# A preamble in another order on VectorE and ScalarE, and the keys' norm table of both layers in one chain

## The chip, the core and the metric

One core of one Trainium2 chip runs the whole program. The metric is the device time of one execution in microseconds; the time of a kernel is the median of its runs. Engines are named as the profile names them: PE is TensorE, DVE is VectorE, ACT is ScalarE, POOL is GpSimd, SP is SyncE, which here only issues DMAs.

## The reference

A trunk of two layers on 512 tokens of width 2048, in float32. Each layer norms its input, makes one input projection, feeds three branches and adds one output projection to the residual stream:

```python
def _layer(x, norm_g, w_in, conv_w, conv_b, sb_qn_g, sb_kn_g, gla_w_up, gla_b_up, gla_on_g, w_out):
    h = _rmsnorm(x, norm_g)
    proj = h @ w_in
    (cv_h, cv_b, cv_c, cv_g, sb_q, sb_k, sb_v, sb_g,
     gl_q, gl_k, gl_v, gl_g, gl_lr) = jnp.split(proj, split_points, axis=-1)
    y_conv = _short_conv(cv_h, cv_b, cv_c, conv_w, conv_b) * silu(cv_g)
    q = _rmsnorm(sb_q.reshape(b, s, SB_HEADS, SB_HD), sb_qn_g)
    k = _rmsnorm(sb_k.reshape(b, s, SB_HEADS, SB_HD), sb_kn_g)
    y_sb = _stick_breaking(q, k, v) * silu(sb_g)
    g = log_sigmoid(gl_lr @ gla_w_up + gla_b_up) / GLA_TAU
    y_gla = _rmsnorm(_gla(gl_q, gl_k, gl_v, g), gla_on_g) * silu(gl_g)
    return x + concatenate([y_conv, y_sb, y_gla]) @ w_out

def _rmsnorm(x, g):
    return x * lax.rsqrt(jnp.mean(x * x, axis=-1, keepdims=True) + EPS) * g
```

The stick-breaking branch has 8 heads of 128; the gated linear attention (GLA) has 4 heads, and its value columns and low-rank columns are the first that the kernel computes.

## The kernel before

**Numbers.** Every float32 factor of a large product is kept as two f16 parts, a high one (`xh`, `wh`) and the residual below it (`xl`, `wl`). A product is three f16 products: high by high, low by high, high by low. Before it is split, a group of weights is scaled by a power of two that comes from its own sum of squares.

**Weight groups.** The weights come in groups of 256 columns in the order of `specs`: per layer 30 groups of `w_in` and 8 of `w_out`. Group 0 is the first half of GLA's values, group 1 the second half with the 16 low-rank columns (tile `kT`), group 2 GLA's queries. A group lands in one of two staging buffers `st` as two halves of 8 blocks of 128 rows (`fetch`, the first three on SP's queue, the others on POOL's). Then, for each group: squares and their sums on ACT (`wmax`, L383; L388 for the narrow columns), a sum over partitions on POOL (L399), four tiny steps to the scale on DVE (`wscale`, L401 to L417), and per half the high part on ACT (`whi`, L454, L456) and the residual on DVE (`wlo`, L461, L464). Group 0 has steps of its own: `wpeak0` (L430 and L433) for its bound, products on PE in place of POOL (L409), and `whi0` (L445 on ACT, L447 on DVE), quarter by quarter.

**Tokens.** The 512 tokens are four tiles of 128. For tile t the preamble makes: the sum of squares (`xsquare`, L630, ACT), the norm's factor (`xnorm`, two steps on ACT and five tiny ones on DVE), the gain, per half of the width (`xgain`, L581, DVE), the transposition of a half by 8 matmuls against the identity into one of two PSUM buffers `psz` (`xhigh`, L591, PE), the copy of that half to f16 `xh` (L593, ACT), and the residual `xl` (`xlow`): for tile 0 PE subtracts the copy in PSUM (L603) and ACT copies (L604), for the other tiles DVE subtracts (L600). A PSUM buffer is free once the residual is made.

**Order.** On DVE and ACT the preamble's steps stand in the order in which the code calls them, from `byhand` (L107) to its end (L684). Everything else, PE included, and DVE's and ACT's later steps among those of the preamble, is placed by a planner, once, when the program is built; an engine then runs its list in order and waits at each step for what the step needs. `order(a, b)` makes the planner put a behind b on one engine, without a wait of its own. The planner deals PE the matmuls of `project_by_token` (L857; groups 0 and 1, all four tiles) between the transposes. Group 2 and what follows is weights by columns (`project_cols`, L702 to L704).

**Around it.** `layer_consts` (L292) turns the small parameters (L294, L295) and makes, for each layer, the table `kg` that the queries of the attention are multiplied by (L1414, near 324 us): a product of two gain vectors, its maximum over partitions on POOL (L183), a power of two below it, a reciprocal, a diagonal, and one product on PE against ones (L310), copied by L311. It is called behind group 0. `xsums` makes sums of token quarters for later products (L735 on DVE, L743 on ACT, 12 and 4 steps in each half of `steps`). `split_v` (L948, L949) takes GLA's values out of PSUM. `weights` (L537) fetches the group two further on.

## Time and profile before

| | us |
|---|---|
| median of 3 runs | 1634.72 |
| lowest and highest | 1633.69, 1635.13 |
| the profiled execution | 1635.55 |
| its span | 1633.8 |

The span runs from the first to the last instruction that the profiler saw; 1.75 us lie around it. A row of a timeline gives the start in the span, the length, the engine, the line, the operation with tiles written and read, the shape, how many instructions are merged in it, and in brackets the engine's idle time before it with what ended that. The length of a matmul counts until its result is out, so the pitch of matmuls is read from start to start. A row of merged instructions can have waits inside it only if they are short.

### The profile page before, as it was taken

To read this page: it belongs to the slowest core of one execution; us is meant where nothing else is said; L and a number is where in the kernel's file an instruction comes from. 1 tells how busy PE (TensorE), PEld (TensorE's weight loads), DVE (VectorE), ACT (ScalarE), POOL (GpSimd) and SP (SyncE) were. 2 spreads that over 40 slices of the span, in tenths; PEclk is the share of its full clock that TensorE was granted. 3 is DMA by queue.
4 is the path that set the end of the run, shared out by engine and by line. 5 is a ranking of instruction groups with operands and counts; after the bars stand their busy time and mean duration, and the time that the engine had idled before them with its cause. 6 is when DMAs were issued, how large, how long until landed. Compare 5 with 4: busy or idle time off the path is not lost.

```text
span 1633.8 us, 42252 instructions
## 1 busy us (share of the span) xinstructions
PE 1615.5 (99%) x18202; PEld 1356.8 (83%) x18202; DVE 1446.2 (89%) x2417; ACT 1196.5 (73%) x1771; POOL 269.4 (16%) x306
## 2 busy tenths in 40 slices
PE   8999999999999999999999999999999999999998
PEld 5757768989899968799996668689898989668998
DVE  7989989989898979898699899898998889898896
ACT  7668887977777776756775697788786868676573
POOL 0122021111212122011102111212121211220110
PEclk9999999999999999999999999999999999999999
DMA  7244435477767686644743544545777786773441
GB/s 262 81 103 145 89 119 111 106 164 144 169 150 169 150 169 186 177 148 147 244 94 107 127 117 103 144 89 137 155 158 160 153 165 150 161 229 130 156 157 54
DMA packets 193643, 235.98 MB, mean 144 GB/s; under 512 B 90242, under 2 KB 153036, under 8 KB 192944
## 3 DMA queue, kind: packets, MB, share of 16 engines
q0 software_dynamic: 79904, 181.42, 42.2%
q1 hardware_dynamic: 104544, 42.42, 13.4%
q10 hardware_dynamic: 9008, 9.45, 1.8%
q8 instruction: 142, 2.33, 0.6%
q14 instruction: 45, 0.37, 0.1%
HBM read 179.65 MB, written 14.68 MB: 119 GB/s over the span
## 4 chain that ended last, share of the span: by engine, by line
PE 68%; DVE 16%; ACT 7%; DMA 5%; issue 3%; POOL 1%; SPq 0%; DVEq 0%; ACTq 0%; POOLq 0%
PE psp L798 22%; PE psp L795 13%; PE psp L857 6%; PE psp L714 4%; PE psp L713 4%; PE psp L715 4%; PE psp L703 3%; PE psp L702 3%; DVE wl L509 3%; PE psp L704 3%; DMA st<-in_w_in_dram 3%; ACT wh L508 1%; PE psm L1345 1%; ACT junk L383 1%; PE psz L1305 1%
## 5 line engine op out<-in xcount | busy, mean ns | idle before, releaser
L508 ACT ACTIVATE wh<-st,ws 128x1024 f16<-128x1024 f32 x270 | 300.7, 1144 | 170.5 <-DVE st L528 89.8
L509 DVE SCALAR_TENSOR_TENSOR wl<-st,ws,wh 128x1024 f16<-128x1024 f32 x270 | 340.3, 1283 | 28.4 <-ACT wh L508 28.3
L383 ACT ACTIVATE junk<-st 128x2048 uint8<-128x2048 f32 x150 | 285.4, 1903 | 14.7 <-DMA st<-in_w_out_dram 6.9
L795 PE MATMUL psp<-s,wh 128*128 128x256 f16 x1280 | 217.7, 273 | 1.0 <-DVE g L811 0.9
L795 PEld LDWEIGHTS <-wh 128*128 128x128 f16 x1920 | 187.4, 98 | 23.3 <-issue 1.4
L798 PE MATMUL psp<-wh,s 128*128 128x128 f16 x2048 | 177.1, 219 | 0.5 <-issue 0.4
L795 PE MATMUL psp<-s,wl 128*128 128x256 f16 x640 | 174.3, 273 | 0.9 <-DVE wl L509 0.9
L713 PE MATMUL psp<-wh,m 128*128 128x256 f16 x640 | 174.5, 273 | 0.0
L715 PE MATMUL psp<-wh,m 128*128 128x256 f16 x640 | 174.5, 273 | 0.0
L714 PE MATMUL psp<-wl,m 128*128 128x256 f16 x640 | 174.5, 273 | 0.0
L798 PEld LDWEIGHTS <-s 128*128 128x128 f16 x3072 | 173.0, 98 | 0.8 <-issue 0.7
L798 PE MATMUL psp<-wl,s 128*128 128x128 f16 x1024 | 173.3, 219 | 0.0
L461 DVE SCALAR_TENSOR_TENSOR wl<-st,ws,wh 128x2048 f16<-128x2048 f32 x62 | 145.0, 2349 | 15.0 <-ACT wh L454 13.8
L362 POOL DMA_DIRECT2D st<-in_w_in_dram x114 | 109.7, 1030 | 246.4 <-DVE w7l L509 118.3
L798 PEld LDWEIGHTS <-m 128*128 128x128 f16 x2448 | 139.1, 98 | 2.1 <-issue 1.6
L454 ACT ACTIVATE wh<-st,ws 128x2048 f16<-128x2048 f32 x60 | 118.6, 1999 | 16.0 <-DVE ws L415 7.9
L399 POOL PARTITION_ALL_REDUCE wgm<-wm x75 | 48.1, 641 | 461.2 <-ACT junk L383 446.0
L386 POOL DMA_DIRECT2D st<-st x36 | 57.2, 1590 | 350.8 <-ACT junk L383 331.5
L795 PEld LDWEIGHTS <-wl 128*128 128x128 f16 x960 | 93.9, 98 | 14.4 <-issue 2.1
L798 PE MATMUL psp<-wh,m 128*128 128x128 f16 x1088 | 97.2, 219 | 0.4 <-DVE ws L415 0.4
L798 PE MATMUL psp<-wl,m 128*128 128x128 f16 x544 | 93.0, 219 | 0.0
L704 PEld LDWEIGHTS <-wl 128*128 128x128 f16 x384 | 37.6, 98 | 44.6
(448 smaller groups left out, 4193.5 us busy)
## 6 DMA issues: line engine op xcount, KB each, us to landing
st<-in_w_in_dram POOLq DMA_DIRECT2D x114, 1024.0 KB, 8.4
st<-in_w_out_dram POOLq DMA_DIRECT2D x32, 1024.0 KB, 8.3
st<-st POOLq DMA_DIRECT2D x36, 512.0 KB, 6.6
st<-in_w_in_dram SPq DMA_DIRECT2D x6, 1024.0 KB, 12.0
mixd<-g POOLq DMA_DIRECT2D x20, 256.0 KB, 7.6
x<-in_x_dram SPq DMA_DIRECT2D x4, 1024.0 KB, 5.2
qT<-in_x_dram ACTq DMA_DIRECT2D x8, 512.0 KB, 4.1
qT<-xs ACTq DMA_DIRECT2D x8, 512.0 KB, 12.2
```

What stands on the lines that cost most here:

```text
L362: load = queue.dma_start(s_, src[l, h * HK * P:(h + 1) * HK * P, c0:c0 + GW].rearrange("(k p) n -> p k n", p=P), max_dma_last_dim=1024)
L383: sq = S.activation(junk(HK * GW).rearrange("p (k n) -> p k n", k=part.shape[1]), part, AF.Square, accum_out=peak[i][:, h:h + 1])
L454: hi = S.activation(wh[:, :, :GW], staged[i][h], AF.Copy, scale=scales[i])
L461: a = V.scalar_tensor_tensor(wl[:, :, :GW], staged[i][h], scales[i], wh[:, :, :GW], ALU.mult, ALU.subtract)
L508: hi = S.activation(h_, b, AF.Copy, scale=sc)
L509: V.scalar_tensor_tensor(l_, b, sc, h_, ALU.mult, ALU.subtract)
L713: T.matmul(o, ah[:, t, k, :], wh[:, kk, :n], start=st_, stop=False, skip_group_check=True)
L714: T.matmul(o, ah[:, t, k, :], wl[:, kk, :n], start=False, stop=False, skip_group_check=True)
L715: return T.matmul(o, al[:, t, k, :], wh[:, kk, :n], start=False, stop=en, skip_group_check=True)
L795: mm = T.matmul(o, w[q_][:, kk, :], a[p_][:, :, kk, :], start=st_, stop=en, skip_group_check=True)
L798: mm = T.matmul(o[:, t * P:(t + 1) * P], a[p_][:, t, kk, :], w[q_][:, kk, :], start=st_, stop=en, skip_group_check=True)
L857: mm = T.matmul(o[:, :n], a_[:, t, k, :], w[k // HK][part][:, k % HK, :n], start=i == 0 and k == 0, stop=i == 2 and k == KT - 1)
```

## The change

Four edits, all in the first layer's preamble and first two groups.

- *Start.* The second half of token tile 0 is copied to f16 by DVE (L602) and not by ACT, ahead of group 0's scale, and the first quarter of group 0's high part is made by DVE, not ACT.
- *Tiles 1 to 3.* The calls stand in another order: squares and norm factors earlier, group 0's second residual (`wlo(0, 1)`) later, gains, transposes and residuals of half tiles in turn, group 1's squares and scale earlier.
- *Constants.* `layer_consts` turns the parameters behind the last transposition, runs one chain of steps for both layers (two columns at a time), and returns a diagonal of both; `key_gains`, called at group 1's second token tile and ordered behind that tile's last matmul, makes both layers' table with one product of 256 columns in a `psz` buffer.
- *Orders.* The first value copy of group 0 goes behind the copy of tile 2's first half on ACT, and the first half of the first layer's token sums (L735, now L746) behind group 1's first residual.

```diff
     def layer_consts():
         pps = bank(psm, "m")
-        T.transpose(pps[:, :NP], prow, ident[:NP, :NP])
+        order(T.transpose(pps[:, :NP], prow, ident[:NP, :NP]), turned[3, 1])
...
-            gq = sm(2, "cm")
-            V.scalar_tensor_tensor(gq[:, 0:1], pcol("qn", l), float(P) ** -0.5, pcol("kn", l), ALU.mult, ALU.mult)
-            V.tensor_scalar(gq[:, 1:2], allmax(gq[:, 0:1], 1, "k"), 2.0 ** -20, None, ALU.max)
-            pow2(zun[:, l:l + 1], gq[:, 1:2], -20.0, "k")
-            V.tensor_scalar(nzun[:, l:l + 1], zun[:, l:l + 1], -1.0, None, ALU.mult)
-            V.reciprocal(gq[:, 1:2], zun[:, l:l + 1])
-            dg = wk([P, P], "e")
-            V.tensor_scalar(gq[:, 0:1], gq[:, 0:1], gq[:, 1:2], 2.0 ** -21, ALU.mult, ALU.mult)
-            V.tensor_scalar(dg, ident, gq[:, 0:1], None, ALU.mult)
-            T.matmul(pps[:, (l + 1) * P:(l + 2) * P], ones.to_broadcast([P, P]), dg, start=True, stop=True)
-            V.tensor_copy(kg[:, l, :], pps[:, (l + 1) * P:(l + 2) * P])
+        gq = sm(depth, "cm")
+        for l in range(depth):
+            V.scalar_tensor_tensor(gq[:, l:l + 1], pcol("qn", l), float(P) ** -0.5, pcol("kn", l), ALU.mult, ALU.mult)
+        gm = allmax(gq, depth, "k")
+        V.tensor_scalar(gm, gm, 2.0 ** -20, None, ALU.max)
+        pow2(zun, gm, -20.0, "k")
+        V.tensor_scalar(nzun, zun, -1.0, None, ALU.mult)
+        V.reciprocal(gm, zun)
+        V.scalar_tensor_tensor(gq, gq, 2.0 ** -21, gm, ALU.mult, ALU.mult)
+        dg = wk([P, depth, P], "e")
+        for l in range(depth):
+            V.tensor_scalar(dg[:, l, :], ident, gq[:, l:l + 1], None, ALU.mult)
+        return dg
+
+    def key_gains(dg, behind):
+        ps = bank2()[:, 0, :depth * P]
+        order(T.matmul(ps, ones.to_broadcast([P, P]), dg.rearrange("p l c -> p (l c)"), start=True, stop=True), behind)
+        V.tensor_copy(kg, ps.rearrange("p (l c) -> p l c", c=P))
...
+        if eng is V:
+            V.tensor_copy(dst[0][:, t, h * HK:(h + 1) * HK, :], ps)
+        else:
+            marks[t, h] = S.activation(dst[0][:, t, h * HK:(h + 1) * HK, :], ps, AF.Copy)
...
     xhigh(0, 0, mix)
     xsquare(1)
+    xhigh(0, 1, mix, V)
     wscale(0)
-    whi0(0, 0, S)
+    whi0(0, 0, V)
     whi0(0, 1, V)
-    xhigh(0, 1, mix)
     whi0(1, 0, V)
...
     xlow(0, 0, mix, True)
     xlow(0, 1, mix, True)
+    xsquare(2)
     wlo(0, 0)
-    wlo(0, 1)
+    xnorm(0, 2)
     xhigh(1, 0, mix)
     xhigh(1, 1, mix)
-    xsquare(2)
     xlow(1, 0, mix, False)
+    xsquare(3)
+    xgain(2, 0)
+    wlo(0, 1)
     xlow(1, 1, mix, False)
-    xnorm(0, 2)
-    xgain(2, 0)
-    xgain(2, 1)
-    xsquare(3)
     xnorm(0, 3)
     xhigh(2, 0, mix)
+    xgain(2, 1)
+    wmax(1, 0)
+    xlow(2, 0, mix, False)
+    xgain(3, 0)
+    wmax(1, 1)
     xhigh(2, 1, mix)
-    wmax(1, 0)
-    xgain(3, 0)
+    wscale(1)
+    xlow(2, 1, mix, False)
+    xhigh(3, 0, mix)
     xgain(3, 1)
-    xlow(2, 0, mix, False)
-    xlow(2, 1, mix, False)
-    wmax(1, 1)
-    wscale(1)
-    xhigh(3, 0, mix)
-    xhigh(3, 1, mix)
     whi(1, 0)
     xlow(3, 0, mix, False)
+    xhigh(3, 1, mix)
+    wlo(1, 0)
     xlow(3, 1, mix, False)
-    wlo(1, 0)
     whi(1, 1)
     wlo(1, 1)
...
             begun = split_v(gv[0], t, o[:, :GW])
-        if l == 0:
-            layer_consts()
+            if not l and not t:
+                order(begun, marks[2, 0])
+        dg = layer_consts() if l == 0 else None
...
             split_v(gv[1], t, o[:, :GW])
+            if not l and t == 1:
+                key_gains(dg, toktail[0])
...
                     order(a, lows[cursor[0] - 1])
+                if not l:
+                    for a in steps[:len(steps) // 2]:
+                        order(a, lows[1])
```

Line numbers below 291 are the same in both kernels; later ones move by 6 to 18.

**At the start.** ACT before, from the copy of tile 0's first half (`x_185` is `xh`, `psz_215` and `psz_242` are the two halves in PSUM, `ssq` the squares' sums, `wh_238` and `wh_252` group 0's two high halves):

```order
L593 ACTIVATE x_185<-psz_215 128x1024
L630 ACTIVATE junk_225,ssq_184<-x_86 128x2048
L445 ACTIVATE wh_238<-st_167,ws_234 128x4x256
L593 ACTIVATE x_185<-psz_242 128x1024
L202 ACTIVATE xr_44_256<-ssq_184,epst 128x1
L205 ACTIVATE xr_44_256<-xr_44_256 128x1
L445 ACTIVATE wh_252<-st_167,ws_234 128x4x256
```

ACT now, the same stretch:

```order
L604 ACTIVATE x_185<-psz_215 128x1024
L641 ACTIVATE junk_225,ssq_184<-x_86 128x2048
L202 ACTIVATE xr_44_256<-ssq_184,epst 128x1
L205 ACTIVATE xr_44_256<-xr_44_256 128x1
L451 ACTIVATE wh_252<-st_167,ws_244 128x4x256
L615 ACTIVATE x_186<-psz_215 128x1024
L615 ACTIVATE x_186<-psz_227 128x1024
```

DVE now, from its part of group 0's bound on:

```order
L439 TENSOR_REDUCE wm_29_208<-st_167 128x1
L602 CAST x_185<-psz_227 128x1024
L416 TENSOR_SCALAR wq_237<-psm_238 128x1
L417 TENSOR_SCALAR wq_237<-wq_237 128x1
L421 TENSOR_SCALAR ws_244<-wq_237 128x1
L423 TENSOR_SCALAR wu_246<-wq_237,inoff_156 128x1
L453 TENSOR_SCALAR wh_248<-st_167,ws_244 128x4x256 x2
L453 TENSOR_SCALAR wh_252<-st_167,ws_244 128x4x256
```

The copy of the second half and the first quarter of the high part have gone from ACT to DVE, and ACT goes from the square of tile 1 straight to its norm.

**At group 1's scale.** DVE before, from the second step of the token sums on (`wq_361`, `ws_367` and `wu_369` are the pieces of group 1's scale, `x_186` is `xl`; `cm` and `kpc` belong to the second layer's table):

```order
L735 TENSOR_TENSOR zw_1135<-x_185,g_1137 128x1024
L402 TENSOR_TENSOR wq_361<-wgm_362 128x1
L302 TENSOR_SCALAR cm_641<-kgm_643 128x1
L735 TENSOR_TENSOR zw_1135<-zw_1135,x_186 128x1024
L411 TENSOR_SCALAR wq_361<-wq_361 128x1
L189 TENSOR_SCALAR kpc_646<-cm_641 128x1
L735 TENSOR_TENSOR zw_1136<-x_185,zw_1135 128x1024
L415 TENSOR_SCALAR ws_367<-wq_361 128x1
L417 TENSOR_SCALAR wu_369<-wq_361,inoff_156 128x1
L600 TENSOR_TENSOR x_186<-psz_371,x_185 128x1024
L190 TENSOR_SCALAR kpc_646<-kpc_646 128x1
L600 TENSOR_TENSOR x_186<-psz_381,x_185 128x1024
```

DVE now, from the first piece of that scale on (`wl_382` is group 1's first residual):

```order
L407 TENSOR_TENSOR wgm_360<-wgm_360 128x1
L961 SCALAR_TENSOR_TENSOR v_407<-psp_464,v_407 128x256
L408 TENSOR_TENSOR wq_359<-wgm_360 128x1
L417 TENSOR_SCALAR wq_359<-wq_359 128x1
L421 TENSOR_SCALAR ws_365<-wq_359 128x1
L423 TENSOR_SCALAR wu_367<-wq_359,inoff_156 128x1
L611 TENSOR_TENSOR x_186<-psz_349,x_185 128x1024
L587 SCALAR_TENSOR_TENSOR x_87<-x_87,xrs_327,g_206 128x1024
L998 TENSOR_SCALAR gu_409<-wu_367 128x1
L611 TENSOR_TENSOR x_186<-psz_370,x_185 128x1024
L467 SCALAR_TENSOR_TENSOR wl_382<-st_173,ws_365,wh_381 128x8x256
```

The token sums (L735, now L746) no longer stand between the scale's pieces or ahead of the residuals of `xl`; the first of them comes behind `wl_382`.

**At tile 2's transposition.** PE now, where tile 2's first half is turned (`psz_329`); before it the low part of tile 1 by the weights, behind it the high part of that same half by the weights:

```order
L868 LDWEIGHTS x_186
L868 MATMUL psp_464<-wh_248,x_186 128x256
L598 MATMUL psz_329<-ident,x_87 128x128 x8
L868 LDWEIGHTS x_185
L868 MATMUL psp_515<-wh_248,x_185 128x256
```

Before, both halves of tile 2 were turned one behind the other ahead of the first matmul that reads either; now the second half is turned 40 matmuls later, together with tile 3's first. Further on, in the attention's first query group, ACT's f16 copy of the queries (L1418) stood behind the two splits of the next weights (L454) and behind the copy L816 that follows them; now it stands ahead of the splits.

The reordering ends in the attention's first group; from there each engine's list is the same as before.

## The prediction

> **What bounds the kernel now.** The page comes first: the span, the busy times and the chain that ended last, by engine.

> ```profile
> span 1633.8 us, 42252 instructions
> PE 1615.5 (99%) x18202; PEld 1356.8 (83%) x18202; DVE 1446.2 (89%) x2417; ACT 1196.5 (73%) x1771; POOL 269.4 (16%) x306
> PE 68%; DVE 16%; ACT 7%; DMA 5%; issue 3%; POOL 1%; SPq 0%; DVEq 0%; ACTq 0%; POOLq 0%
> ```

> TensorE (PE) is the bound, and only 18.3 us of the span are not PE. The next view gives the busy times by stage: the start, the rest of the preamble with the first two weight groups, the stage up to 340 us, and all that follows. The columns are the stretch, its length, then busy time of PE, weight loads, VectorE (DVE), ScalarE (ACT) and GpSimd, the granted clock and the DMA share.

> ```profile
> 0.00:20.00 20.00, 13.84 (x48) 8.09 (x49) 11.90 (x43) 16.39 (x22) 2.10 (x6) 1.00 0.93 334
> 20.00:54.00 34.00, 31.29 (x260) 26.39 (x259) 33.11 (x65) 27.20 (x35) 1.33 (x3) 1.00 0.41 119
> 54.00:340.00 286.00, 284.99 (x2842) 214.35 (x2841) 263.37 (x507) 221.66 (x344) 53.58 (x60) 1.00 0.46 118
> 340.00:1634.00 1294.00, 1285.37 (x15057) 1107.97 (x15055) 1137.84 (x1804) 931.25 (x1372) 212.37 (x239) 1.00 0.61 148
> ```

> PE idles 6.2 us in the first stretch, 2.7 in the second, and 1.0 in the third. The reordering reaches no further than about 340 us, so only these three stretches can move. The PE timeline of the first two (start, length, line, tiles; in brackets the idle time before and what ended it) shows where:

> ```profile
> 11.22 3.68 PE L591 MATMUL psz<-ident,x 128*128 128x128 f32 x16 [1.60 <-DVE x L581]
> ...
> 15.82 1.01 PE L603 MATMUL psz<-x,ga 128*128 128x512 f16 x2
> 18.11 1.87 PE L857 MATMUL psp<-wh,x 128*128 128x256 f16 x8 [1.27 <-ACT wh L445]
> 19.77 1.06 PE L603 MATMUL psz<-x,ga 128*128 128x512 f16 x2
> 20.62 3.20 PE L857 MATMUL psp<-wh,x 128*128 128x256 f16 x16
> 23.66 1.04 PE L591 MATMUL psz<-ident,x 128*128 128x128 f32 x8
> 24.54 1.04 PE L857 MATMUL psp<-wh,x 128*128 128x256 f16 x8
> 25.41 1.04 PE L591 MATMUL psz<-ident,x 128*128 128x128 f32 x8
> ...
> 35.71 1.96 PE L857 MATMUL psp<-wh,x 128*128 128x256 f16 x16 [0.24 <-ACT x L593]
> 38.86 1.09 PE L591 MATMUL psz<-ident,x 128*128 128x128 f32 x8 [1.19 <-DVE x L600]
> ...
> 46.91 3.03 PE L857 MATMUL psp<-wh,x 128*128 128x256 f16 x24 [0.62 <-DVE kpc L190]
> ...
> 52.32 2.94 PE L857 MATMUL psp<-wh,x 128*128 128x272 f16 x24 [0.64 <-ACT wh L456]
> ```

> Two things are to be seen. There are five waits: 1.27 at the start, then 0.24, 1.19, 0.62 and 0.64. And PE has two speeds: 8 matmuls of 128x256 take 1.66 from 18.11 to 19.77 (0.208 each) but 0.87 from 24.54 to 25.41 (0.109). The 16 from 20.62 to 23.66 take 3.04, which is about 13 slow and 3 fast ones, so the speed doubles near **23.3**. The clock column says 1.00 for all stretches; the halved speed is only in the durations.

> **The change, part by part.**

> *Start.* ACT and DVE rows around the first matmul, then the nearest rows for the new DVE copy:

> ```profile
> 15.02 1.91 ACT L630 ACTIVATE junk<-x 128x2048 uint8<-128x2048 f32 x1 [0.28 <-DMA x<-in_x_dram]
> 16.93 1.13 ACT L445 ACTIVATE wh<-st,ws 128x1024 f16<-128x1024 f32 x1
> 16.00 0.16 DVE L410 TENSOR_SCALAR wq<-psm 128x1 f32<-128x1 f32 x1 [2.31 <-PE psm L409]
> 16.57 1.41 DVE L447 TENSOR_SCALAR wh<-st,ws 128x1024 f16<-128x1024 f32 x2
> 38.84 1.22 DVE L600 TENSOR_TENSOR x<-psz,x 128x1024 f16<-128x1024 f32 x1
> 34.63 1.94 ACT L593 ACTIVATE x<-psz 128x1024 f16<-128x1024 f32 x2 [0.49 <-PE psz L591]
> ```

> The first split of the weights waits on ACT behind the square of token tile 1 (15.02 to 16.93), though its scale was ready at 16.57. After the change DVE makes it. DVE also copies the second half of tile 0: its transposes are done by about 14.9, the copy has no row of its own and lies between ACT's 0.97 and DVE's 1.22 for the same size; I take 1.22, the same engine. It ends at 16.1, inside DVE's idle 2.31, so the scale comes 0.1 late; the first split (half of 1.41) ends near 17.4. PE meanwhile runs both L603 pairs on end: 15.82 plus twice 0.85 (19.77 to 20.62) is 17.52, then the matmuls. Before, that point, both pairs done, was worth 18.11 + 0.85 = 18.96. The lead of 1.44 is slow work, so **0.72** at full speed.

> *Clock.* The one rise in the trace came 23.3 - 18.1 = 5.2 us after PE began to work without a wait. From 11.22 to 16.6 it also worked without a wait, mostly at transposes, and the clock did not rise. After the change the unbroken f16 work begins at 15.82, 2.3 earlier; a rise 2.3 earlier is worth half, **1.15**. The bounds are nothing (the rise stays at 23.3) and (23.3 - 17.5)/2 = 2.9 (no slow matmul left). I take 1.15, as the only rise measured. [...]

> *The other four waits.* The rows that made them, on DVE, and the cost of one batch of transposes on PE (23.66 to 24.54, 0.87):

> ```profile
> 35.21 2.46 DVE L581 SCALAR_TENSOR_TENSOR x<-x,xrs,g 128x1024 f32<-128x1024 f32 x2
> 37.59 1.22 DVE L600 TENSOR_TENSOR x<-psz,x 128x1024 f16<-128x1024 f32 x1
> 40.16 1.22 DVE L735 TENSOR_TENSOR g<-x,x 128x1024 f32<-128x1024 f16 x1
> 44.31 1.22 DVE L735 TENSOR_TENSOR zw<-x,zw 128x1024 f32<-128x1024 f16 x1
> 45.45 0.15 DVE L415 TENSOR_SCALAR ws<-wq 128x1 int32<-128x1 int32 x1
> 45.63 1.22 DVE L600 TENSOR_TENSOR x<-psz,x 128x1024 f16<-128x1024 f32 x1
> ```

> The 1.19 is PE waiting for a PSUM buffer, because the residual of tile 2 (L600, 37.59) stood behind both gains of tile 3 (L581). The 0.62 and 0.64 come from DVE having run four steps of the token sums (L735, 40.16 to 45.4) between the pieces of group 1's scale and ahead of tile 3's residuals (L600, 45.63). The change holds the first layer's sums behind group 1's first residual and interleaves gains and residuals; DVE, 33.11 of 34.00 busy here, is relieved of some 1.13 a step. These three waits go.

> New ones come: PE now turns tile 1's halves together and needs the copy at once, as at 35.71 (0.24), and again with tile 2's second half; and it turns tile 2's first half alone, without the 0.87 of a second batch as cover, so 0.24 + 0.87 = 1.11. Each wait also costs the last matmul's draining, its length less its pitch: 1.04 for 8 against 0.87, 0.17. Before: 0.24 + 1.19 + 0.62 + 0.64 + 4 x 0.17 = 3.37. After: 0.24 + 0.24 + 1.11 + 3 x 0.17 = 2.10. The gain is **1.27**; bounds are 3.37 (none of the new waits) and a loss of 0.47 (all three bare).

> *Keys' table.* The chain of waits has the two products of the table, and two are replaced by one twice as wide:

> ```profile
> 65.57 0.22 PE psm L310 x2
> ```

> That is 0.22 each before and 0.44 once after: nothing. The ten or so tiny DVE steps (0.15 each) are halved; DVE covers them. The one product now stands some 20 matmuls into group 2, about 4 us of cover, for a chain whose last link on DVE stands ahead of group 2's second residual, which PE needs later still.

> *Queues.* Group 0's second residual moves behind tile 2's first gain, and with it the fetch of group 2 on SP, from 29.20 to some 31. Its readers:

> ```profile
> 29.20 1.01 SPq L362 DMA_DIRECT2D st<-in_w_in_dram  x2
> 48.10 1.90 ACT L383 ACTIVATE junk<-st 128x2048 uint8<-128x2048 f32 x1
> ```

> The next reader, the squares on ACT, began 18.9 after the issue; 17 are left, and PE needs what comes of them only in group 2. I take nothing; if ACT came 7 us earlier and the landing bound it, the squares would wait, not PE. POOL gives up one of two all-reduces: nothing.

> *54 to 340 us.* The list of PE's waits there (total, times, longest):

> ```profile
> PE psp L795 <- DVE wl L509: 0.4, 1, 0.4
> PE psp L798 <- DVE ws L415: 0.4, 1, 0.4
> ```

> The planner deals these steps out anew. I take nothing; bounds are a gain of 0.8 and a loss of 1.04 (ACT's copy of the first queries, below).

> **The sum.** 0.72 + 1.15 + 1.27 = 3.1 us. The profiled execution took 1635.55, so 1632.4; the median of the runs shown, 1634.72, is 0.83 below that execution, so **1631.6**.

> **The rivals.**

> *The clock rises no earlier* (it keeps its distance from the program's start). For it: one rise is one sample. Then 0.72 + 1.27 = 2.0, 1632.7.

> [...]

> *It does not do what it says*: DVE, at 97% in the preamble, only hands the waits on, the new waits come bare (a loss of 0.47), and the clock stays. Then 0.72 - 0.47, 1634.5.

> *Slower.* At 324 us ACT now has the copy of the first queries (L1418) ahead of both weight splits, and the copy that frees PE's bank (L816) behind them:

> ```profile
> 324.28 3.90 ACT L454 ACTIVATE wh<-st,ws 128x2048 f16<-128x2048 f32 x2 [0.18 <-DVE ws L415]
> 328.09 0.36 ACT L816 ACTIVATE kT<-psp 128x256 f32<-128x256 f32 x1
> 328.35 1.04 ACT L1418 ACTIVATE qp<-raw 128x1024 f16<-128x1024 f32 x1
> ```

> If PE arrives there when ACT has only begun, it waits 1.04 + 3.90 = 4.9, and the sum is 1.8 slower, 1636.5; it decides once that wait passes 3.1. Against it: before, PE came late enough to wait for none of it.

> **Chances.** Forecast 0.45 (its own range 1631.0 to 1632.2), no earlier rise 0.2, a whole stretch 0.2, no effect 0.08, slower 0.07. The range reaches from the clock's and the waits' better ends to just short of no effect, with 0.4 for the spread of the runs: 1630.0 to 1634.0. A measurement of this kernel can tell about 0.2%, 3.3 us; the bound, 1631.45, lies inside the forecast's own range, so that gives faster 0.42, same 0.50, slower 0.08.

> **What would show it.** The first matmul of group 2 before:

> ```profile
> 73.97 0.38 PE L702 MATMUL psp<-x,wh 128*128 128x512 f16 x1
> ```

> In the new trace: the first matmul of group 0 (L857, now L868) near 17.5 with no wait before it; a change of pitch from 0.21 to 0.11 near 21; in the preamble three waits, about 0.24, 1.1 and 0.24, all on ACT's copy; that matmul (now L713) at 71 or just under; the single product of the table without a wait before it; idle time of PE between 54 and 340 us of about 1. The prediction is wrong if PE waits on DVE in the preamble, if the pitch changes at 23 or later, or if a wait over 1 us stands near 324.

## The result and the profile after

| | before | after |
|---|---|---|
| median, us | 1634.09 (9 runs) | 1629.59 (9 runs) |
| lowest and highest | 1633.09, 1635.13 | 1628.41, 1631.67 |
| the profiled execution | 1635.55 | 1631.67 |

The ratio of the times is 0.9976, 95% interval 0.9967 to 0.9985: 3.9 us faster by the ratio (2.5 to 5.4), 4.5 by the medians. Forecast were 3.1 us and 1631.6; the direction and the size are within the interval. The median lies 0.4 below the stated range, but the kernel before, timed beside it, was 0.6 faster than its 1634.72 as well: 3.9 off that 1634.72, from which the forecast started, is 1630.8, inside it. The way to it was another one in three steps. The profiled execution of the changed kernel is the slowest of its nine. (Of the executions of the kernels below, one, of the changed kernel with 15 throwaway products, took 8572 us for a reason that the record does not show; its ratio leaves it out.)

The page of the changed kernel, its span, busy times and the chain that ended last by engine:

```profile
span 1629.8 us, 42246 instructions
PE 1612.1 (99%) x18200; PEld 1353.9 (83%) x18200; DVE 1447.0 (89%) x2411; ACT 1196.4 (73%) x1769; POOL 272.8 (17%) x305
PE 71%; DVE 15%; ACT 7%; DMA 3%; issue 3%; POOL 0%; SPq 0%; DVEq 0%; ACTq 0%; POOLq 0%
```

PE is still the bound, with 17.7 us of the span not PE's, and 71% of the chain where it had 68. The busy times by stage, with the columns of before (the last stage ends 4 us earlier with the span):

```profile
0.00:20.00 20.00, 13.95 (x61) 7.91 (x62) 14.77 (x47) 16.49 (x22) 2.11 (x6) 1.00 0.91 335
20.00:54.00 34.00, 32.07 (x286) 27.96 (x285) 33.49 (x57) 26.52 (x36) 3.86 (x5) 1.00 0.46 134
54.00:340.00 286.00, 285.20 (x2844) 214.06 (x2842) 265.73 (x516) 225.39 (x343) 54.78 (x57) 1.00 0.48 119
340.00:1630.00 1290.00, 1280.85 (x15016) 1103.92 (x15013) 1132.98 (x1794) 928.04 (x1369) 212.08 (x237) 1.00 0.60 148
```

PE is hardly less idle ahead of 54 us: 6.05 + 1.93 = 8.0 against 6.2 + 2.7 = 8.9. From 54 to 340 us it idles 0.8 (before 1.0), behind that 9.2 (8.6). But ahead of 54 us it did 347 matmuls instead of 308. The PE timeline shows how:

```profile
11.01 3.35 PE L598 MATMUL psz<-ident,x 128*128 128x128 f32 x16 [1.36 <-DVE x L587]
...
15.68 0.59 PE L614 MATMUL psz<-x,ga 128*128 128x512 f16 x2 [0.30 <-DVE x L602]
16.91 2.36 PE L868 MATMUL psp<-wh,x 128*128 128x256 f16 x16 [0.64 <-DVE wh L453]
19.57 1.96 PE L868 MATMUL psp<-wh,x 128*128 128x256 f16 x16 [0.30 <-ACT x L615]
...
23.84 1.05 PE L868 MATMUL psp<-wh,x 128*128 128x256 f16 x8 [0.57 <-ACT x L604]
...
29.50 1.05 PE L868 MATMUL psp<-wh,x 128*128 128x256 f16 x8 [1.12 <-ACT x L604]
...
36.03 3.67 PE L868 MATMUL psp<-wh,x 128*128 128x256 f16 x32 [0.24 <-ACT x L604]
...
69.05 0.38 PE L713 MATMUL psp<-x,wh 128*128 128x512 f16 x1
```

The 16 transposes take 3.35 us and not 3.68: instruction by instruction their pitch drops from 213 to 109 ns at **13.89 us**, amid the transposes. Before, that came at 23.25. The f16 matmuls of group 0 begin at full speed, and six waits, 3.17 us in all, stand between 15 and 37 us. Group 2 begins 73.97 - 69.05 = **4.92** us earlier; 0.44 of it is the keys' product, which now stands behind that point. Of the other 4.48 the last matmul, at 1625.03 for 1629.01, still has 3.98: a wait at 403 us is 0.9 longer in this execution (1.41, before 0.52), while waits elsewhere are shorter.

The order can also be seen on ACT, in the four high parts of group 1. Before:

```profile
45.63 2.00 ACT L454 ACTIVATE wh<-st,ws 128x2048 f16<-128x2048 f32 x1 [0.27 <-DVE ws L415]
...
51.88 0.39 ACT L456 ACTIVATE wh<-kT,ws 128x128 f16<-128x128 f32 x1
```

After:

```profile
36.77 2.00 ACT L460 ACTIVATE wh<-st,ws 128x2048 f16<-128x2048 f32 x1
...
47.23 0.39 ACT L462 ACTIVATE wh<-kT,ws 128x128 f16<-128x128 f32 x1
```

The first of them comes 8.9 us earlier, the last 4.7. Before, PE waited 0.64 for the last of them (at 52.32); in the changed kernel it waits for none.

### The profile page after: what moved, and what is told of

It is laid out like the page before. It is cut to its first block, busy times and chain, and to the rows that moved or that the text cites. A ratio compares the mean times of both kernels' runs of the same rounds, so it can differ in the third digit from the quotient of the medians.

```text
span 1629.8 us, 42246 instructions
## 1 busy us (share of the span) xinstructions
PE 1612.1 (99%) x18200; PEld 1353.9 (83%) x18200; DVE 1447.0 (89%) x2411; ACT 1196.4 (73%) x1769; POOL 272.8 (17%) x305
## 4 chain that ended last, share of the span: by engine, by line
PE 71%; DVE 15%; ACT 7%; DMA 3%; issue 3%; POOL 0%; SPq 0%; DVEq 0%; ACTq 0%; POOLq 0%
PE psp L809 22%; PE psp L806 12%; PE psp L868 6%; PE psp L726 5%; PE psp L725 5%; PE psp L724 5%; PE psp L714 4%; PE psp L713 4%; PE psp L715 3%; DVE wl L515 3%; DMA st<-in_w_in_dram 1%; ACT wh L514 1%; PE psm L1363 1%; ACT junk L389 1%; PE psz L1323 1%
## 5 line engine op out<-in xcount | busy, mean ns | idle before, releaser
L389 ACT ACTIVATE junk<-st 128x2048 uint8<-128x2048 f32 x150 | 285.5, 1903 | 16.3 <-DMA st<-in_w_in_dram 8.6
L405 POOL PARTITION_ALL_REDUCE wgm<-wm x75 | 51.6, 689 | 458.6 <-ACT junk L389 430.9
```

The lines of the kernel that those rows point to most:

```text
L389: sq = S.activation(junk(HK * GW).rearrange("p (k n) -> p k n", k=part.shape[1]), part, AF.Square, accum_out=peak[i][:, h:h + 1])
```

## The experiments

Each kernel was timed side by side with the kernel before. In the table, the difference is worked out from the ratio (of 1634 us), with its interval; beside it are, from the profiled execution, the point at which PE's pitch halves and the first matmul of group 2. One execution's end differs by a microsecond or two for waits behind 340 us, so that point tells more of the preamble than the time. The product or products of the keys' table, 0.44 us, stand ahead of that point in all these kernels but the changed one, the one without the start and the two changed ones with throwaway products (behind it there); in the one without the new table half of it stands ahead.

| kernel | us against before | pitch halves at | group 2 at |
|---|---|---|---|
| before | | 23.25 | 73.97 |
| changed | -3.9 (-5.4 to -2.5) | 13.89 | 69.05 |
| before + start | -0.5 (-2.0 to +0.8) | 20.07 | 72.44 |
| before + sums' order | -1.6 (-3.1 to -0.2) | 23.14 | 72.01 |
| before + constants | -0.2 (-1.6 to +1.1) | 15.09, lost 18.50, 21.92 | 72.42 |
| before + 12 throwaway products | +0.7 (-0.8 to +2.1) | 22.60 | 73.62 |
| before + 28 throwaway products | +0.7 (-0.8 to +2.1) | 12.87 | 72.84 |
| changed - start | -2.9 (-4.4 to -1.5) | 22.36 | 70.32 |
| changed - sums' order | -3.1 (-4.6 to -1.6) | 19.79 | 70.40 |
| changed - late turn of parameters | -2.8 (-4.2 to -1.5) | 18.94 | 70.30 |
| changed - new table | +0.2 (-1.3 to +1.5) | 14.58 | 69.08 |
| changed - all constants | +4.6 (+2.6 to +6.4) | 15.45 | 70.31 |
| changed + 12 throwaway products | -4.2 (-5.9 to -2.6) | 13.14 | 69.25 |
| changed + 15 throwaway products | -3.9 (-5.4 to -2.5) | 14.46 | 69.02 |

### The start alone, and the sums' order alone

```diff
     xsquare(1)
+    xhigh(0, 1, mix, V)
     wscale(0)
-    whi0(0, 0, S)
+    whi0(0, 0, V)
     whi0(0, 1, V)
-    xhigh(0, 1, mix)
```

> The kernel before with the change's start alone: DVE copies the second half of tile 0 ahead of group 0's scale and makes the first quarter of group 0's high part. Theory A (behind the start, ACT and DVE set the pace of the preamble before, up to the wait for group 1's high part at 52.3 us, and PE's own slow work there is largely covered by waits): the first f16 matmul of group 0 comes near 17 instead of 18.1, the waits behind it grow, and no more than 0.3 to 0.7 us of the 1.4 reach the end: 1633.4 to 1633.8 against 1634.1. Rival B (PE's own work is the bound, and the earlier start brings the clock's rise forward as the prediction had it): 0.72 + 1.15 = 1.9 faster, 1632.2.

The time can't tell A from no change (-2.0 to +0.8); B's 1.9 lies at the edge of the interval. The PE timeline of this run has a new wait:

```profile
28.81 0.25 PE L294 MATMUL psm<-ident,e 42*128 42x42 f32 x1 [0.88 <-DMA e<-in_gla_on_g_dram]
...
38.13 1.09 PE L591 MATMUL psz<-ident,x 128*128 128x128 f32 x8 [1.31 <-DVE x L603]
```

PE came earlier than the parameters had landed, and the wait for DVE's residual grew from 1.19 to 1.31.

```diff
                 for a in steps[len(steps) // 2:]:
                     order(a, lows[cursor[0] - 1])
+                if not l:
+                    for a in steps[:len(steps) // 2]:
+                        order(a, lows[1])
```

> The kernel before, with one thing of the change: the first half of the first layer's token sums ordered behind group 1's first residual. Theory A (DVE's sums between the pieces of group 1's scale and ahead of tile 3's residuals are what PE waits for at 46.9 and 52.3): both waits, 0.62 and 0.64 with their 0.17 of draining, go, and DVE's relief shortens the wait at 38.9 as well: 1.3 to 2 us faster, 1632.1 to 1632.8. Rival B (the gain of the change is the clock's earlier rise, and waits taken away come back elsewhere): within 0.5 of 1634.1.

A, as far as time tells: 1.6 faster, and both waits are gone from the PE timeline. The one at 38.9 stays, though, at its old length; A had it shorter.

```profile
38.79 1.09 PE L591 MATMUL psz<-ident,x 128*128 128x128 f32 x8 [1.19 <-DVE x L600]
...
72.01 0.38 PE L702 MATMUL psp<-x,wh 128*128 128x512 f16 x1
```

### An earlier clock, by throwaway products

```diff
     for h in range(2):
-        spread(h)
+        spent = spread(h)
+    idle = bank(psp, "p")
+    for _ in range(12):
+        order(T.matmul(idle[:, :P], identb, identb, start=True, stop=True), spent)
```

> The kernel before, with 12 throwaway products of 128x128 bf16 in PE's idle time from 9.4 to 11 us, so that PE is busy without a break from before 9.5 to 16.6 us; their result is not used. If what PE does decides when its pitch halves, it halves by 16.3 at the latest in every execution, not at 23.3. Theory A (before, the preamble is held by ACT and DVE up to 52.3 us, so a faster PE only waits longer): the time stays within 0.5 us of 1634.1, with more idle time of PE ahead of 54 us. Rival B (PE's slow work is the bound, 7 us of it lie between 16.3 and 23.3): about 3.5 us faster, 1630.6, and with it nearly the whole gain of the change.

> The changed kernel with the same 12 throwaway products ahead of its transposes. Theory A (the changed order lets PE run as fast as it can, and the changed kernel's spread of 3.3 us between runs, against 2.0 before, comes from the clock rising now early, now late): the rise comes between 12.9 and 16.3 in every execution, the runs close up to about 1.5 us, and the median moves to the fast end of the changed kernel's runs, 1628.4 to 1629.3. Rival B (the changed kernel's clock always rises as early as the 13.9 us of its one profile): no difference from 1629.6, and the spread stays.

In the kernel before, the 12 products failed to bring the rise forward (22.60), so that run did not test what an early rise is worth. The 12.9 and 16.3 of the two texts are the author's estimate, 9.5 plus once and twice 3.41, the difference of the times at full clock in the traces of before and changed (1611.09 and 1614.50); the rise at 22.60 shows that 16.3 is no latest time. In the changed one the rise came at 13.14, inside the span. Its median, 1628.93, lies where theory A had it, but the kernel before, timed beside it, was 0.8 faster as well; by the ratio the time is not to be told from the changed kernel's, and its runs lay 2.6 us apart (1627.53 to 1630.13) instead of the 1.5 of theory A. A second pair of runs made the work denser: 15 products here, and for the kernel before 13 more behind the first subtraction.

```diff
-            T.matmul(ps[:, i:i + 4, :], negi, xh[:, i:i + 4, :], start=False, stop=True, skip_group_check=True)
+            mm = T.matmul(ps[:, i:i + 4, :], negi, xh[:, i:i + 4, :], start=False, stop=True, skip_group_check=True)
+        if (t, h) == (0, 0):
+            for _ in range(13):
+                order(T.matmul(idle[:, :P], identb, identb, start=True, stop=True), mm)
```

> The changed kernel with 15 throwaway products of 128x128 bf16 in PE's idle time ahead of the transposes (12 in the earlier run); their result is not used. By the reading that the clock rises at the end of a stretch of 3.41 us with more than about 72% of wide work, wide work from 9.5 to 14.3 us makes the rise come between 11.9 and 15.3 wherever the stretches lie. Theory A (the clock's rise is a matter of where the stretches lie, and the changed kernel loses by a late one): rise in that span, 4.4 to 5.2 us faster than before, the fast end of what the changed kernel showed. Rival B (no more to be had from the clock): 3.9 to 4.4 faster, as the changed kernel.

The rises came in the spans named (12.87 and 14.46). The kernel before then runs at full speed from 12.87 on, 10.4 us earlier than in its own trace, and its PE timeline shows what becomes of it:

```profile
14.68 0.59 PE L607 MATMUL psz<-x,ga 128*128 128x512 f16 x2 [0.24 <-ACT x L597]
...
17.89 1.03 PE L864 MATMUL psp<-wh,x 128*128 128x256 f16 x8 [1.88 <-ACT wh L449]
...
20.25 0.60 PE L864 MATMUL psp<-wh,x 128*128 128x256 f16 x4 [0.43 <-ACT wh L449]
21.17 1.05 PE L864 MATMUL psp<-wh,x 128*128 128x256 f16 x8 [0.32 <-ACT x L611]
...
72.84 0.38 PE L709 MATMUL psp<-x,wh 128*128 128x512 f16 x1
```

PE's waits between 14 and 22 us are 2.87, where the kernel before has 1.27, and a wait of 0.38 for the parameters is new at 28.71. Group 2 begins 1.13 earlier; theory A had nothing, B 2 to 4. The time shows no gain. For the changed kernel B held: no more to be had that these times can tell.

### The constants alone

```diff
-        T.transpose(pps[:, :NP], prow, ident[:NP, :NP])
+        order(T.transpose(pps[:, :NP], prow, ident[:NP, :NP]), turned[3, 1])
...
+        dg = layer_consts() if l == 0 else None
...
+            if not l and t == 1:
+                key_gains(dg, toktail[0])
```

(with the one chain of the change in `layer_consts`)

> The kernel before with the change's constants alone: the parameters turned behind the last transposition, one chain for both layers, one product in group 1. Theory A (the constants are a gain in themselves: fewer tiny steps on DVE at 97% in the preamble, no waits of PE for the parameters): group 2 begins 1 to 2 us earlier than 73.97 and the kernel is 1 to 2 us faster than before. Rival B (they count only where the new order would else be hurt): within 0.5 of before.

The time is B's, group 2's 72.42 is A's: not settled. It told something else. Its busy times over four stretches of 3.41 us, the distance of its clock's changes at 15.09, 18.50 and 21.92 (the granted clock is the third number from the right; ahead of the first change that a trace holds it reads 1.00, whatever the pitch: so from 0 to 20 us before, at a pitch of 213 ns) and its PE timeline in the second of them:

```profile
11.68:15.09 3.41, 3.41 (x18) 3.41 (x17) 1.87 (x2) 3.01 (x5) 0.00 (x0) 1.00 1.03 426
15.09:18.50 3.42, 1.06 (x7) 0.66 (x8) 2.04 (x8) 3.19 (x4) 0.00 (x0) 1.00 1.01 422
18.50:21.92 3.42, 3.42 (x15) 2.12 (x14) 2.06 (x6) 3.38 (x6) 0.00 (x0) 0.50 1.04 345
21.92:25.30 3.38, 3.38 (x32) 3.17 (x31) 3.38 (x3) 1.65 (x2) 0.00 (x0) 1.00 1.14 323
```

```profile
15.46 0.59 PE L611 MATMUL psz<-x,ga 128*128 128x512 f16 x2
18.41 1.80 PE L865 MATMUL psp<-wh,x 128*128 128x256 f16 x8 [2.35 <-ACT wh L451]
```

The clock rose at 15.09, after transposes. With the old start PE then waited 2.35 us for ACT's first split; the stretch had 1.06 us of work in its 3.42, and the next ran at half speed, busy as it was.

### The changed kernel with one part undone

```diff
-    xhigh(0, 1, mix, V)
     wscale(0)
-    whi0(0, 0, V)
+    whi0(0, 0, S)
     whi0(0, 1, V)
+    xhigh(0, 1, mix)
```

> The changed kernel with its start undone: ACT copies the second half of tile 0, behind group 0's scale, and makes the first quarter of group 0's high part. Theory A (the start alone brought the kernel before 0.03%, since the waits behind it took the rest; with the waits gone it counts): 0.7 to 1.5 us slower than the changed kernel, that is 2.7 to 3.7 faster than before. Rival B (the start never counts): the changed kernel's time, 4.2 to 4.5 faster than before. Rival C (the start is the core of the change): 3 us or more of the 4.4 are lost.

A by the ratios: 1.0 slower than the changed kernel, though the intervals overlap. It is the cleanest view of the new order without the two start effects, since its start (18.17) and its clock (22.36) are nearly those of before:

```profile
18.17 1.86 PE L868 MATMUL psp<-wh,x 128*128 128x256 f16 x8 [1.49 <-ACT wh L451]
...
37.30 3.67 PE L868 MATMUL psp<-wh,x 128*128 128x256 f16 x32 [0.37 <-ACT x L604]
...
70.32 0.38 PE L713 MATMUL psp<-x,wh 128*128 128x512 f16 x1
```

Of the waits behind the start one is left, 0.37, and group 2 begins 3.65 earlier than before.

```diff
-                if not l:
-                    for a in steps[:len(steps) // 2]:
-                        order(a, lows[1])
```

> The changed kernel without the order that holds the first half of the first layer's token sums behind group 1's first residual. Theory A (that order alone made the kernel before 1.6 us faster, and it is as much worth here): the waits for group 1's scale and tile 3's residuals come back, and the kernel is 1 to 2 us slower than the changed one, 2 to 3 faster than before. Rival B (group 1's squares and scale now stand early enough): the changed kernel's time, 4 faster than before.

0.8 slower than the changed kernel by the ratios, between A and B, and the intervals overlap. One wait of 0.43 for DVE's residual comes back at 45.97.

```diff
-        order(T.transpose(pps[:, :NP], prow, ident[:NP, :NP]), turned[3, 1])
+        T.transpose(pps[:, :NP], prow, ident[:NP, :NP])
```

> The changed kernel without one order: the turning of the parameters on PE is not held behind the last transposition, so it stands where it stood before, amid the second token tile's transposes and products. In the kernel before the parameters' DMAs landed at 29.7 us and PE came at 29.9; with the start alone PE came earlier and waited 0.88 for them. Theory A (the landing does not move with the change): PE comes near 27.5, waits 1 to 2.3 us for the landing, and the kernel is slower than the changed one by 0.7 to 2 us, 2.4 to 3.7 faster than before. Rival B (the prediction's reading: where the constants stand costs nothing): 4.2 to 4.5 faster than before, as the changed kernel.

1.1 slower by the ratios, as A had it, again with overlapping intervals. The wait is there in the PE timeline, 0.72 where A had 1 to 2.3; the parameters had landed by 28.10 here, not at 29.7, so A's premise that the landing does not move failed:

```profile
28.10 0.22 PE L294 MATMUL psm<-ident,e 42*128 42x42 f32 x1 [0.72 <-DMA e<-in_conv_w_dram]
...
30.46 1.05 PE L868 MATMUL psp<-wh,x 128*128 128x256 f16 x8 [1.12 <-ACT x L604]
```

For all constants as before, the edit is the one of "The constants alone", reversed:

> The changed kernel with all constants as before: parameters turned early, one chain and one product of the table for each layer, called behind group 0, none of it held back on PE. Theory A (of the constants only the turn of the parameters counts): as the run without that order, within 0.7 us. Rival B (the table's chain on DVE, twice as many tiny steps, or the list that the planner then makes, counts too): slower than that run by over 1 us, with new waits of PE on DVE behind the preamble. Rival C (nothing in the constants counts): the changed kernel's time.

B, and by far: slower than before by 4.6 us. The last run left the turn of the parameters late and put back the table alone (in `layer_consts` the two chains and products in `pps`, and no `key_gains`):

> The changed kernel with the keys' table alone as before: one chain and one product for each layer, in the psm bank of the parameters, called behind group 0; the turning of the parameters stays held behind the last transposition. Of the two runs before this, which differ by the table alone, the one with the old table was 8 us slower (1638.05 against 1630.05), and its trace has waits of PE on DVE behind the preamble (2.7 at 123 us, 1.4 at 194, others near 1 at 177 and 333). Theory A (the two chains push the low-rank steps back on DVE, and weight splits come late for PE): group 2 begins within 0.5 us of 69.1, waits of 2 us or so follow near 120 and 190, and the kernel is slower than the changed one by 3 to 8 us: from 1 faster to 4 slower than before. Rival B (it needed the early turn too): the changed kernel's time, 4 faster than before.

A: group 2 begins at 69.08, as in the changed kernel, and by the ratios all of the gain is lost behind it. (The two profiled executions differ by 1.2 only, spans of 1631.0 and 1629.8: PE idles 4.2 more between 54 and 340 us with the old table, but 1.9 less behind 340, and the changed kernel's is the slowest of its nine.) Busy times of PE between 54 and 340 us are 281.04, where the changed kernel has 285.20. PE's products into the small bank `psm`, then the DVE rows that matter:

```profile
68.51 0.39 PE L310 MATMUL psm<-e,ones 128*128 128x128 f32 x2
92.82 0.39 PE L310 MATMUL psm<-e,ones 128*128 128x128 f32 x2
97.58 0.39 PE L989 MATMUL psm<-identb,qT 128*128 128x128 bf16 x4
```

```profile
93.24 0.29 DVE L311 COPY kg<-psm 128x128 f32<-128x128 f32 x1 [1.15 <-PE psm L310]
...
98.00 0.69 DVE L993 CAST e<-psm 128x512 bf16<-128x512 f32 x1 [2.38 <-PE psm L989]
...
121.66 0.69 DVE L1005 TENSOR_TENSOR ga<-ga,za 128x512 f32<-128x512 f32 x1
122.85 1.29 DVE L509 SCALAR_TENSOR_TENSOR w7l<-st,ws,w7h 128x1024 f16<-128x1024 f32 x1
124.38 1.37 DVE L1008 TENSOR_TENSOR_SCAN raw<-ones,ga 128x128 f32<-128x128 f32 x4
```

In the changed kernel these rows are (PE's first low-rank product, then DVE):

```profile
77.25 0.22 PE L996 MATMUL psm<-identb,qT 128*128 128x128 bf16 x1
```

```profile
90.60 0.69 DVE L1000 CAST e<-psm 128x512 bf16<-128x512 f32 x1
...
105.18 0.68 DVE L1012 TENSOR_TENSOR ga<-ga,za 128x512 f32<-128x512 f32 x1
106.12 1.36 DVE L1015 TENSOR_TENSOR_SCAN raw<-ones,ga 128x128 f32<-128x128 f32 x4
```

There is one `psm` buffer. The parameters and both table products sit in it until the second table is copied, at 93.24; the products that turn the low-rank columns need the same buffer and begin at 97.58 and not at 77.25. The gate's second half (L1005, L1008) lands at 122 to 126, amid the weight splits (L509), and these are what PE waits for; the list of PE's waits from 54 to 340 us:

```profile
PE psp L800 <- DVE zw L816: 2.5, 1, 2.5
PE psp L800 <- DVE wl L509: 1.9, 1, 1.9
PE psz L1135 <- DVE zw L1121: 0.5, 1, 0.5
```

In the kernel before, the second table product ran at 65.41, ahead of the low-rank columns (68.99), and the buffer cost nothing. The pair of kernels shows that the table decides some 4 us in the new order (the intervals, -5.4 to -2.5 and -1.3 to +1.5, do not overlap). That it does so through the buffer is not shown: it is read from these rows, and the old chains with a buffer of their own were not tried. The run with all constants old speaks against the buffer as the only cause. There it was free by 72.3, the first low-rank product came at 77.86, and yet the waits are similar (2.71 at 123.3, 1.41 at 193.5): the low-rank steps stand later in DVE's list as well (the copy out of `psm` at 96.2, not 90.6), for a reason that stays open. What the two kernels with the old table in the new order share is that DVE does the gate's second half 10 and 16 us later than in the changed kernel (105.18), amid the weight splits; with all constants old:

```profile
115.16 0.68 DVE L1005 TENSOR_TENSOR ga<-ga,za 128x512 f32<-128x512 f32 x1
```

## Why the prediction was right, and where it was not

**Start: the reading held where the clock was low.** With the clock still down, the first matmul of group 0 comes at 17.18 and 17.22 without a wait (in the changed kernels without the sums' order and without the late turn); 17.5 was said:

```profile
17.18 4.94 PE L868 MATMUL psp<-wh,x 128*128 128x256 f16 x32
17.22 4.50 PE L868 MATMUL psp<-wh,x 128*128 128x256 f16 x32
```

Where the clock is up already, PE is faster than DVE, and the waits for DVE that the text named as a sign of error appear (0.30 at 15.68 and 0.64 at 16.91).

**Clock, 1.15: the failed step.** In one trace the clock was still down at 16.6, although PE had worked without a wait from 11.22; from that the prediction left the transposes out and let the rise follow f16 work by 5.2 us. In the changed kernel's trace the clock rose at 13.89 with nothing but transposes in the 3.41 us behind it, at a point that the change does not reach. All that PE did there is 2.88 us, 14 transposes (columns as in the busy times by stage):

```profile
10.48:13.89 3.41, 2.88 (x14) 2.88 (x15) 2.89 (x3) 3.38 (x6) 1.11 (x1) 1.00 1.06 408
```

Counted back in steps of 3.41 us from the rise, the stretches lie elsewhere in each of the two traces. In the kernel before, the one from 13.01 to 16.42 was busy throughout, but only 67% of it with transposes and other wide matmuls; the rest are L409's products with a single column, and no rise came at 16.42. So the rise at 13.89 was no effect of the change to be priced at 2.3 us earlier.

Where the rise came only behind the transposes, the change does bring it forward, by a whole stretch of 3.41 us to within 0.2; the prediction gave that a chance of 0.2. In two pairs whose stretches lie within 0.1 us of each other, the rise goes from 22.36 (changed without the start) to 18.94 (without the late turn), and from 23.14 (before with the sums' order) to 19.79 (changed without it). With the start alone, in the order before, it goes from 23.25 to 20.07, with stretches 0.2 apart. The hole ahead of group 0 is closed; in the run with the constants alone, where it was 2.35 us long, the clock that had risen at 15.09 fell again at 18.50. With the rise at 18.94 the prediction's way of adding comes near: 0.72 + (23.25 - 18.94)/2 + 1.27 is 4.1, and group 2 came 73.97 - 70.30 = 3.7 earlier, 4.6 without that kernel's own wait of 0.72 and its draining, 0.17.

A rise earlier still is worth less than its slow matmuls: 10.4 us earlier gave the kernel before 1.13 us at group 2. For the changed kernel, take the two with the new start and a late rise (18.94 and 19.79). In both the keys' product, 0.44, runs ahead of group 2; in the one without the late turn:

```profile
58.74 0.59 PE L317 MATMUL psz<-e,ones 128*128 128x256 f32 x2
```

70.30 less 0.72, 0.17 and 0.44 is 69.0; 70.40 less its wait of 0.43, 0.17 and 0.44 is 69.4. Against 69.05, the early rise is worth between nothing and 0.3 there.

**The other four waits, 1.27: right for one place of PE, and without a fixed size.** In the two kernels just named the new waits on ACT's copy are 0.24, 1.12 and 0.24, as priced. In the changed trace, where PE is earlier, they are 0.57, 1.12 and 0.24, and one of 0.30 at 19.57 comes on top: from 3.37 (with draining) to 2.91, a gain of 0.46. With the start undone and a late clock only one of 0.37 is left: from 3.37 to 0.37 + 0.17 is 2.8. There group 2 comes 3.65 earlier, less 0.44 for the moved product 3.2; the rise 0.9 earlier explains up to 0.45 of the difference. The step priced waits and slow matmuls as if both could be saved. They are the same slack against ACT and DVE: what one gives up the other takes. Added to the kernel without the start, start and clock together brought 70.32 - 69.05 = 1.27 where 1.87 were said. The errors go in opposite directions, whichever way they are shared out, and the sum came out 1.3 low at group 2 (3.14 against 4.48, of which up to 0.2 is that the transposes began at 11.01 and not 11.22, ahead of all that changed). That the forecast still covers the time is in part luck.

**Keys' table, nothing: right from kernel to kernel, wrong as a reading.** In the old order the new constants move the time by nothing that can be told (-0.2), and in the changed kernel PE waits for nothing that comes of the table. But the table left as before costs the new order 4.1 us by the ratios, all the gain. The prediction counted the products and DVE's tiny steps and asked whether DVE covers them. It did not ask where the new order would put the old chains, what they would hold there, and which later steps on DVE would move.

**54 to 340 us, nothing: right, but only with the new table.** PE idles 0.80 there, before 1.01; with the old table 4.96. The slower rival's wait near 324 us is 0.27.

**Queues, nothing: right** as far as the trace tells: nothing waits for group 2's fetch. The parameters, which the text left out, do count: turned early, they make PE wait 0.72 for their landing.

Not settled: how the 3.9 splits between the order of the tiles and that of the sums, since each single part moves the time by about as much as a measurement can tell, and the clock of each profiled run differs; and by which steps the old table delays the gate's second half.

## What to carry to other kernels

When a step is moved, follow what hangs on it far behind it, the buffers that it holds and the next to need them too, besides its own instructions: a table of 0.44 us of products decided some 4 us by what came 50 us later. (In that run it held the one buffer that others needed 27 us longer than before; whether that was the cause stays open.) When several engines are near their limit, waits and slow work of one are not two gains; read the sum at one point behind the stage, such as the first matmul of the next group. A term that depends on when the clock rises should be given as a span, not from one trace: the last rises of these 14 traces lie between 12.87 and 23.25.

## What the runs showed of the hardware

The granted clock is full from the last rise to the fall at the end for 1611.09 us in the trace of the kernel before (from 23.25) and for 1614.50 in that of the changed kernel (13.89 to 1628.39): 3.41 apart. With the constants alone its changes at 15.09, 18.50 and 21.92 stand 3.41 and 3.42 apart, and between the last two it reads 0.50. The transposes of tile 0 have a pitch of 213 ns in the kernel before and, up to the rise, in the changed kernel; behind it they have 109.

Looked at in stretches of 3.41 us back from a rise, the one that ends in it was filled with transposes and other wide matmuls to 84% in the changed kernel (10.48 to 13.89, transposes alone), 87% with the constants alone (11.68 to 15.09), 95% in the changed kernel without the new table (11.17 to 14.58), 99% in the one without the late turn (15.53 to 18.94), and 100% in the one without the sums' order (16.38 to 19.79) and in the kernel before (19.84 to 23.25). Three stretches of 67% were not followed by a rise, though PE was busy throughout with its products with a single column counted: 13.01 to 16.42 in the kernel before, 12.12 to 15.53 without the late turn, 12.97 to 16.38 without the sums' order. What happens between 67% and 84%, these stretches do not show; the 71 to 83% (from six traces) and the 72% of the two expectations are the author's estimate. The prediction left the transposes out of what the rise follows; in the changed kernel the rise at 13.89 came after a stretch in which PE did nothing else.
